# A decoder layer on one core: squares of x added by the matmul engine in the opening, other visit thresholds in the projections

## The chip, the core and the metric

The kernel runs on one core of a Trainium2 chip. In the profile PE is the matmul engine (PEld its weight loads), DVE the vector engine, ACT the scalar engine, POOL the general one, and SP the queue that issues nearly all DMAs. The metric is device time in microseconds (us) for one launch. Each engine works through its own list of instructions strictly in order, and waits where an operand or a buffer isn't ready; the lists are fixed when the program is built.

## The reference

One layer for 256 tokens of width 2048, all in float32:

```python
mod = jax.nn.silu(c) @ w_ada[l] + b_ada[l]
shift1, scale1, gate1, shift2, scale2, gate2 = jnp.split(mod, 6, axis=-1)
h = modulate(rms_norm(x, g_norm1[l]), shift1, scale1)   # h*(1+scale)+shift
p = h @ w_in[l]                                         # 2048 -> 12288
# retention on q,k,v,g and HGRN2 on q,f,i,g, both in chunks of 128 tokens,
# head norms, two output projections, gates, w_out
x = x + gate1[:, None, :] * (merged @ w_out[l])
h2 = modulate(rms_norm(x, g_norm2[l]), shift2, scale2)
u = causal_depthwise_conv(h2 @ w_up[l], conv_w[l], conv_b[l])
a, bgl = jnp.split(u, 2, axis=-1)
x = x + gate2[:, None, :] * ((jax.nn.silu(a) * bgl) @ w_down[l])
return rms_norm(x, g_final)
```

## The kernel before, in words

The width is cut into 16 pieces of 128, called k. A product with a float32 weight is made of three faster products: ACT copies a loaded weight tile `raw` into a rounded upper part `wh` (L176), DVE subtracts to get the rest `wl` (L181), and PE adds wh times the upper and the lower part of the activation and wl times the upper part. A tile pair wh, wl normally holds two k's by 512 columns. The pool `raw` has 11 buffers, and `wh` and `wl` have 4 each. All loads of weights stand in one queue, SP's, in the order of the program.

**The opening** (lines 305 to 430). The conditioning vector c is transposed on PE, put through Silu on ACT (L328, tile `col`), and spread over all partitions by 16 small matmuls in four groups of four (`spread`, L339, PSUM tiles `po`); ACT copies each group to the tile `sc` (L415, L427). Meanwhile x arrives transposed, in four tiles `xT`. Each is squared, folded and summed over the width by matmuls with a column of ones (`sums`, L375), which give the squared sum of each token in a `po` tile. `token_rstd` (L390, L391) takes the root on ACT and the reciprocal on DVE, and PE spreads the result (L395). For the root ACT needs another function table than for Silu; `sqrt_table` loads it (L402). Matmuls on ones (`idle`, L248) fill PE where it would stand. The tag `po` has four PSUM buffers: the fourth group of `spread` gets the buffer of the first, and waits until ACT has copied that one.

**Modulation.** The scale and the shift of one k are dot products of `sc` with rows of the conditioning weights: `ada_dot`, one `SCALAR_TENSOR_TENSOR` of 1024 elements a half on DVE (L507). For k=0 there are five of them (the last half is cut in two); the first two give the scale, the other three the shift. `times` multiplies x by the reciprocal (L497), `opening` makes z (L896), and `summed` makes h (L887). With h of k=0 PE begins the real products (`mm_plain`, L231). A second round of five dots leads to h of k=1 and to `mm_apart` (L242). All of this is pinned: it runs in the order in which it is written.

**The visits.** The projections to 14 column groups of 512 (`ATT`) begin before all k's are modulated. A planner (`visits`) goes round the groups; each visit takes the k's that a group has not yet had, and the number of k's that count as ready rises with the work done (a constant, one k for every 11 units). Groups 0 and 1 keep their PSUM banks to the end; every other visit ends with `take`: ACT copies the bank to SBUF the first time (L880), DVE adds it later (L882). The remaining dots, two scale and two shift dots for a k, run beside the visits. From here on nothing is pinned: a list scheduler decides the order on each engine, from its own estimate of when things are ready, when the program is built. After the visits come the heads, the output projections, the second norm, the convolution and the down projection; the change does not touch them.

Of the kernel before, what the change touches and what calls it, by code (L numbers as in the profile page):

```python
# [34 lines left out]
ADA_EVERY = 11  # L35
LAG = 2
NOSYNC = mybir.DependencyInfo(mybir.DependencyClass.NoSync, mybir.DependencyReason.DATA)
# [23 lines left out]
class Kernel:  # L61
# [106 lines left out]

    def upper(self, src, m, w, gain=None, shift=(0, 0)):

        raw = self.load(src, m, w)
        if gain is not None:
            self.pin(self.nc.vector.tensor_tensor(raw, raw, gain[:, None, :].to_broadcast([P, m, w]), ALU.mult))
        self.n += 1
        wh, wl = [self.part(n, m, w, at) for n, at in zip(("wh", "wl"), shift)]
        self.pin(self.nc.scalar.activation(wh, raw, AF.Copy))  # L176
        return raw, wh, wl
# [6 lines left out]

    def pieces(self, src, kts, gain=None, shift=(0, 0)):

        uppers = []
        for k in range(0, kts, 2):
            m = min(2, kts - k)

            while len(uppers) <= k // 2 + (gain is not None) and 2 * len(uppers) < kts:
                at = 2 * len(uppers)
                z = min(2, kts - at)
                uppers.append(self.upper(src[:, at : at + z, :], z, G, gain, shift))
# [48 lines left out]

    def idle(self, n):

        ps = self.pg()[0]
        for _ in range(n):
            self.pin(self.nc.tensor.matmul(ps[:, :P], lhsT=self.ones, rhs=self.ones, start=True, stop=True))  # L248

# [55 lines left out]
    def constants(self):  # L305
# [79 lines left out]
    def token_rstd(self, ps):  # L385
# [8 lines left out]
        for t in range(NT):  # L394
            self.pin(nc.tensor.matmul(ps[:, t * P : (t + 1) * P], lhsT=q[:, t : t + 1].to_broadcast([P, P]), rhs=self.ident, start=True, stop=True))  # L395
        self.idle(9)
        return ps
# [6 lines left out]
    def norm_x(self):  # L404

        nc = self.nc
        self.xT = self.load_x()
        ps = self.po()[:, :NT]
        for i, x in enumerate(self.xT):
            z = self.blk([P, 4, T], name="sq")  # L410
            if i == 0:
                self.pin(nc.vector.tensor_tensor(z, x, x, ALU.mult))
            elif i < 3:
                self.pin(nc.scalar.activation(z, x, AF.Square))
                self.pin(nc.scalar.activation(*self.silu.pop(0), AF.Copy))  # L415
            else:
                self.pin(nc.scalar.activation(z[:, :2, :], x[:, :2, :], AF.Square))
                self.pin(nc.vector.tensor_tensor(z[:, 2:, :], x[:, 2:, :], x[:, 2:, :], ALU.mult))
            if i < 3:
                self.pin(nc.vector.tensor_tensor(z[:, :2, :], z[:, :2, :], z[:, 2:, :], ALU.add))  # L420
                self.pin(nc.vector.tensor_tensor(z[:, 0, :], z[:, 0, :], z[:, 1, :], ALU.add))
            self.sums(ps, [z[:, j, :] for j in range(1 if i < 3 else 4)], i == 0, i == 3)
            if i == 0:
                for u in (2, 3):
                    self.spread(u)
        for part in self.silu:
            self.pin(nc.scalar.activation(*part, AF.Copy))  # L427
        return ps
# [417 lines left out]
    def run(self):  # L846
# [53 lines left out]
        gen = first(0)  # L900
        for _ in range(2):
            next(gen)
        rx = self.token_rstd(parts)
        rx_sb = c.tile([P, T], F32, name="rx_sb")
        next(gen)
        self.times(0, 1, rx)
        self.pin(nc.scalar.activation(rx_sb, rx, AF.Copy))
        z = opening(0)
        for _ in gen:
            pass  # L910
# [8 lines left out]
        for g in range(RESIDENT, FIRST):  # L919
            if g == RESIDENT:  # L920
                self.pin(nc.scalar.activation(hi, h, AF.Copy))
            uppers.append(self.upper(a["wa"][g][:, 0:1, :], 1, G))
        self.pin(nc.vector.tensor_tensor(lo, h, hi.bitcast(F32), ALU.subtract))
# [12 lines left out]
        for _ in gen:  # L936
            pass
        uppers = [self.upper(a["wa"][g][:, 1:2, :], 1, G) for g in range(RESIDENT)]
        hi, lo = act(1)[:, :T], act(1)[:, T:]
# [6 lines left out]
        for g in range(RESIDENT, FIRST):  # L946
            wh, wl = self.rest(self.upper(a["wa"][g][:, 1:2, :], 1, G))
            mms[g](ps[g], [(act(1), wh[:, 0, :], wl[:, 0, :])], False, True)
        begun = list(self.pieces(a["wa"][FIRST][:, 0:2, :], 2))
        for _ in range(2):  # L950
            next(ada[2])
# [446 lines left out]
```

## Time and profile before

| what | value |
|---|---|
| time, median of 3 runs | 1504.68 us (1504.5 to 1504.94) |
| time of the profiled execution | 1503.57 us |
| its span, first to last instruction | 1501.8 us |
| PE busy | 1485.5 us, 99% |
| DVE busy | 1210.5 us, 81% |
| ACT busy | 839.8 us, 56% |
| first real product (L231) starts at | 18.43 us |
| PE idle between 100 and 500 us | 2.34 us |

Times inside the profile count from the first instruction. A matmul of the opening in float32 shows as two passes, so eight matmuls of `sums` are 16 instructions there. A row of the timeline gives the start, the duration, the engine, the line, the tile written and the tiles read, and, in brackets, how long the engine stood before it and what ended that. Rows that follow each other with the same text are merged and counted.

### The profile page before, as it was taken

The numbers are of one execution on the slowest core, as the hardware profiler recorded it, in microseconds if no ns is written. First come the engines' busy times: TensorE is split into PE (matmuls) and PEld (weight loads), VectorE is DVE, ScalarE is ACT, GpSimd is POOL, SyncE is SP. The second block draws the span as 40 slices with busy tenths as digits, with TensorE's granted clock in tenths as the row PEclk, the third lists the DMA queues.
The fourth block names the chain that finished last, engine by engine and source line by source line (L and its number), as shares of the span: only waits on it lengthen the run. The fifth ranks groups of instructions, "written<-read, shape, count | busy, mean of one in ns | idle before, by whom it ended". The sixth has DMA issues, their size and how long they took to land.

```text
span 1501.8 us, 22826 instructions
## 1 busy us (share of the span) xinstructions
PE 1485.5 (99%) x8537; PEld 1274.6 (85%) x8537; DVE 1210.5 (81%) x1654; ACT 839.8 (56%) x1211; POOL 4.0 (0%) x8
## 2 busy tenths in 40 slices
PE   8999999999999999999999999999999999999997
PEld 7888889888888888888888888888888888888886
DVE  7899997999999877898978778778777769455694
ACT  5645546867775644445466555555555558344342
POOL 0000000000000000000000000000000000000000
PEclk9999999999999999999999999999999999999999
DMA  9999997688887889989847777777777666666551
GB/s 371 370 308 350 350 324 262 210 290 279 278 284 263 281 298 325 312 293 363 306 132 241 249 232 234 233 235 237 232 245 234 221 188 208 195 210 212 178 185 56
DMA packets 111455, 385.73 MB, mean 257 GB/s; under 512 B 12864, under 2 KB 13424, under 8 KB 111344
## 3 DMA queue, kind: packets, MB, share of 16 engines
q1 hardware_dynamic: 110448, 383.14, 76.3%
q8 instruction: 67, 1.10, 0.3%
q10 hardware_dynamic: 896, 1.13, 0.2%
q14 instruction: 44, 0.36, 0.1%
HBM read 382.11 MB, written 2.11 MB: 256 GB/s over the span
## 4 chain that ended last, share of the span: by engine, by line
PE 90%; DVE 5%; ACT 2%; DMA 1%; issue 1%; DVEq 0%; ACTq 0%; SPq 0%
PE pg L205 12%; PE pg L210 12%; PE pg L206 12%; PE po L1231 11%; PE pg L1231 11%; PE po L1233 5%; PE pg L1233 5%; PE pg L255 4%; PE po L206 3%; PE po L205 3%; PE po L210 3%; DVE wl L181 2%; PE pg L258 2%; DVE raw L507 1%; DVE p L882 1%
## 5 line engine op out<-in xcount | busy, mean ns | idle before, releaser
L181 DVE TENSOR_TENSOR wl<-raw,wh 128x1024 fp32r<-128x1024 f32 (+1 forms) x535 | 631.2, 1190 | 225.4 <-ACT wh L176 217.2
L176 ACT ACTIVATE wh<-raw 128x1024 fp32r<-128x1024 f32 (+1 forms) x535 | 545.8, 1032 | 468.1 <-PE pg L206 185.2
L507 DVE SCALAR_TENSOR_TENSOR raw<-raw,sc 128x1024 f32<-128x1024 f32 (+2 forms) x194 | 233.5, 1209 | 0.0
L205 PE MATMUL pg<-wh,hT 128*128 128x512 f32 x512 | 202.4, 396 | 3.7 <-ACT wh L176 2.6
L206 PE MATMUL pg<-wh,hT 128*128 128x512 f32 x512 | 199.8, 390 | 0.0
L1231 PE MATMUL po<-h2T,wh 128*128 128x512 f32 x704 | 175.8, 392 | 0.0
L1231 PE MATMUL pg<-h2T,wh 128*128 128x512 f32 x688 | 172.1, 392 | 0.0
L1231 PEld LDWEIGHTS po<-h2T,wh 128*128 128x128 f32 x704 | 125.7, 188 | 21.7
L1231 PEld LDWEIGHTS pg<-h2T,wh 128*128 128x128 f32 x688 | 122.8, 188 | 21.2
L210 PE MATMUL pg<-wl,hT 128*128 128x512 f32 x512 | 138.9, 390 | 0.3 <-DVE wl L181 0.3
L205 PEld LDWEIGHTS pg<-wh,hT 128*128 128x128 f32 x512 | 96.1, 188 | 25.3 <-ACT wh L176 4.9
L210 PEld LDWEIGHTS pg<-wl,hT 128*128 128x128 f32 x512 | 95.9, 188 | 21.0 <-DVE wl L181 0.9
L206 PEld LDWEIGHTS pg<-wh,hT 128*128 128x128 f32 x512 | 96.2, 188 | 19.4 <-DVE hT L436 0.3
L1233 PEld LDWEIGHTS po<-h2T,wl 128*128 128x128 f32 x704 | 93.4, 188 | 7.5
L1233 PEld LDWEIGHTS pg<-h2T,wl 128*128 128x128 f32 x688 | 91.3, 188 | 7.3
L1233 PE MATMUL po<-h2T,wl 128*128 128x256 f32 x704 | 94.5, 277 | 0.0
L1233 PE MATMUL pg<-h2T,wl 128*128 128x256 f32 x688 | 92.5, 277 | 0.0
L206 PE MATMUL pg<-wh,gs 128*128 128x512 f32 x176 | 68.6, 390 | 0.0
L205 PE MATMUL pg<-wh,gs 128*128 128x512 f32 x176 | 68.5, 389 | 0.0
L205 PE MATMUL po<-wh,gs 128*128 128x512 f32 x176 | 68.5, 389 | 0.0
L206 PE MATMUL po<-wh,gs 128*128 128x512 f32 x176 | 68.5, 389 | 0.0
L1244 ACT ACTIVATE u<-uy,convw 128x256 f32<-128x256 f32 x88 | 52.4, 595 | 28.7 <-DVE uy L1242 28.4
(273 smaller groups left out, 2033.9 us busy)
## 6 DMA issues: line engine op xcount, KB each, us to landing
raw<-in_wup SPq DMA_DIRECT2D x176, 512.0 KB, 4.5
raw<-in_wdown SPq DMA_DIRECT2D x88, 512.0 KB, 4.1
raw<-in_wa SPq DMA_DIRECT2D x79, 512.0 KB, 5.5
raw<-in_ada SPq DMA_DIRECT2D x64, 512.0 KB, 5.6
raw<-in_wab SPq DMA_DIRECT2D x64, 512.0 KB, 5.2
raw<-in_ada SPq DMA_DIRECT2D x62, 512.5 KB, 5.6
raw<-in_gate SPq DMA_DIRECT2D x32, 512.5 KB, 4.8
raw<-in_wk SPq DMA_DIRECT2D x32, 512.0 KB, 4.9
```

Of the source, the lines that this page charges most:

```text
L176: self.pin(self.nc.scalar.activation(wh, raw, AF.Copy))
L181: self.last = self.nc.vector.tensor_tensor(wl, raw, wh.bitcast(F32), ALU.subtract)
L205: nc.tensor.matmul(ps[t], lhsT=act[:, hi], rhs=wh, start=first and i == 0, stop=False)
L206: nc.tensor.matmul(ps[t], lhsT=act[:, lo], rhs=wh, start=False, stop=False)
L210: nc.tensor.matmul(ps[t], lhsT=act[:, hi], rhs=wl, start=False, stop=last and i == len(items) - 1)
L255: nc.tensor.matmul(ps[z], lhsT=wh[:, z * P : (z + 1) * P], rhs=act, start=first and i == 0, stop=False)
L258: nc.tensor.matmul(ps[z][:, :T], lhsT=wl[:, z * P : (z + 1) * P], rhs=act[:, :T], start=False, stop=last and i == len(items) - 1)
L507: dot = self.pin(nc.vector.scalar_tensor_tensor(raw[:, 0, :], raw[:, 0, :], 1.0, self.sc[:, at:to], ALU.mult, ALU.mult, accum_out=part[:, ...
L882: nc.vector.tensor_tensor(dst, dst, z, ALU.add)
L1231: self.pin(nc.tensor.matmul(ps[z], lhsT=wh[:, z * P : (z + 1) * P], rhs=act, start=kt == 0, stop=False, skip_group_check=bool(begun)))
L1233: nc.tensor.matmul(ps[z][:, :T], lhsT=wl[:, z * P : (z + 1) * P], rhs=act[:, :T], start=False, stop=kt == KT - 1, skip_group_check=bool(be ...
L1244: nc.scalar.activation(u, y, AF.Identity, bias=w[3], scale=w[2])
```

## The change

In the opening the order is written anew. The four squares are made as follows: tile 0 on DVE, folded twice; tile 1 on ACT, folded twice; tiles 2 and 3 half on ACT and half on DVE, tile 2 folded once and tile 3 not at all, so that PE sums two parts of tile 2 (four matmuls) and four of tile 3 (eight). The load of the root's table moves from behind Silu to behind the square of tile 1. `token_rstd` comes after one dot of k=0 where it came after two; the second dot follows the reciprocal, and the third follows the product with x. One filler matmul fewer stands after the spread of the reciprocal, and two new ones that read z stand before the first product. The first tiles of groups 2 and 3, and of 0 and 1 for k=1, get an offset of 8 bytes in their buffers (`COLS`), as later visits have. The weights of the second and third visit (`stock`) are loaded ahead of the dots of k=2. The thresholds of readiness are a table: 14, 24, 34, 45, ... units of work for k = 2, 3, 4, 5, ..., where the formula gave 13, 24, 35, 46, ... The plan has 46 visits where it had 47.

```diff
-LAG = 2
+READY = (14, 24, 34, *range(45, 156, 11))
...
-    def upper(self, src, m, w, gain=None, shift=(0, 0)):
+    def upper(self, src, m, w, gain=None, shift=(0, 0), raw=None):
-        raw = self.load(src, m, w)
+        raw = raw or self.load(src, m, w)
...
         self.pin(nc.scalar.activation(col, ps, AF.Silu))
-        self.sqrt_table()
...
-        self.idle(9)
+        self.idle(8)
         return ps
...
         ps = self.po()[:, :NT]
-        for i, x in enumerate(self.xT):
-            z = self.blk([P, 4, T], name="sq")
-            if i == 0:
-                self.pin(nc.vector.tensor_tensor(z, x, x, ALU.mult))
-            elif i < 3:
-                self.pin(nc.scalar.activation(z, x, AF.Square))
-                self.pin(nc.scalar.activation(*self.silu.pop(0), AF.Copy))
-            else:
-                self.pin(nc.scalar.activation(z[:, :2, :], x[:, :2, :], AF.Square))
-                self.pin(nc.vector.tensor_tensor(z[:, 2:, :], x[:, 2:, :], x[:, 2:, :], ALU.mult))
-            if i < 3:
-                self.pin(nc.vector.tensor_tensor(z[:, :2, :], z[:, :2, :], z[:, 2:, :], ALU.add))
-                self.pin(nc.vector.tensor_tensor(z[:, 0, :], z[:, 0, :], z[:, 1, :], ALU.add))
-            self.sums(ps, [z[:, j, :] for j in range(1 if i < 3 else 4)], i == 0, i == 3)
-            if i == 0:
-                for u in (2, 3):
-                    self.spread(u)
-        for part in self.silu:
-            self.pin(nc.scalar.activation(*part, AF.Copy))
+        zs = [self.blk([P, 4, T], name="sq") for _ in self.xT]
...
+        times(zs[0], self.xT[0])
+        fold(zs[0], 2)
+        fold(zs[0], 1)
+        self.pin(act(zs[1], self.xT[1], AF.Square))
+        self.sqrt_table()
+        fold(zs[1], 2)
+        fold(zs[1], 1)
+        self.sums(ps, [zs[0][:, 0, :]], True, False)
+        for u in (2, 3):
+            self.spread(u)
+        self.sums(ps, [zs[1][:, 0, :]], False, False)
+        for i in (2, 3):
+            self.pin(act(zs[i][:, low, :], self.xT[i][:, low, :], AF.Square))
+            times(zs[i][:, high, :], self.xT[i][:, high, :])
+            if i == 2:
+                fold(zs[i], 2)
+            spread_out()
+            self.sums(ps, [zs[i][:, j, :] for j in range(2 * i - 2)], False, i == 3)
+        while self.silu:
+            spread_out()
...
-        for _ in range(2):
-            next(gen)
+        next(gen)
         rx = self.token_rstd(parts)
         rx_sb = c.tile([P, T], F32, name="rx_sb")
         next(gen)
         self.times(0, 1, rx)
         self.pin(nc.scalar.activation(rx_sb, rx, AF.Copy))
+        next(gen)
         z = opening(0)
+        self.idle(2, z)
...
-            uppers.append(self.upper(a["wa"][g][:, 0:1, :], 1, G))
+            uppers.append(self.upper(a["wa"][g][:, 0:1, :], 1, G, shift=COLS))
...
         begun = list(self.pieces(a["wa"][FIRST][:, 0:2, :], 2))
+        stock = {g: self.load(a["wa"][g][:, 0:2, :], 2, G) for g in range(FIRST + 1, FIRST + 3)}
...
-                have = min(KT, 2 + int((work - LAG) / ADA_EVERY))
+                have = 2 + sum(work >= at for at in READY)
...
-            pieces = self.pieces(a["wa"][g][:, k : k + m, :], m, shift=visit(g))
+            pieces = self.pieces(a["wa"][g][:, k : k + m, :], m, shift=visit(g), raw=stock.pop(g, None))
```

How the lists of the engines move is shown at three places. A row is a line of the kernel, the operation, the tile written, the tiles read and the size.

The first place is the opening. On ACT, from Silu (`col`) to the copies of `sc`, before:

```order
L328 ACTIVATE col_99<-po_95 128x16
L402 ACT_TABLE_LOAD
L402 ACTIVATE warm_101<-eps_71 128x1
L414 ACTIVATE sq_138<-xT_114 128x1024
L415 ACTIVATE sc<-po_103 128x512
L414 ACTIVATE sq_145<-xT_115 128x1024
L415 ACTIVATE sc<-po_108 128x512
L417 ACTIVATE sq_152<-xT_116 128x512
```

And with the change:

```order
L328 ACTIVATE col_99<-po_95 128x16
L424 ACTIVATE sq_121<-xT_112 128x1024
L401 ACT_TABLE_LOAD
L401 ACTIVATE warm_128<-eps_71 128x1
L433 ACTIVATE sq_122<-xT_113 128x512
L419 ACTIVATE sc<-po_101 128x512
L433 ACTIVATE sq_123<-xT_114 128x512
L419 ACTIVATE sc<-po_106 128x512
```

Ahead of the first copy to `sc` there are now a square of 1024, the table, and a square of 512, where there were the table and a square of 1024. On DVE, from the last square to h of k=0, before:

```order
L418 TENSOR_TENSOR sq_152<-xT_116 128x512
L507 SCALAR_TENSOR_TENSOR raw_182,dot_32_181<-raw_182,sc 128x1024
L507 SCALAR_TENSOR_TENSOR raw_185,dot_32_181<-raw_185,sc 128x1025
L391 RECIPROCAL rq_191<-rq_191 128x2
L507 SCALAR_TENSOR_TENSOR raw_211,dot_39_210<-raw_211,sc 128x1024
L497 TENSOR_TENSOR xT_113<-xT_113,po_194 128x256
L507 SCALAR_TENSOR_TENSOR raw_218,dot_39_210<-raw_218,sc 128x512
L507 SCALAR_TENSOR_TENSOR raw_221,dot_39_210<-raw_221,sc 128x513
L887 TENSOR_SCALAR h_224<-z_216,dot_39_210 128x256
```

And with the change:

```order
L413 TENSOR_TENSOR sq_123<-xT_114 128x512
L520 SCALAR_TENSOR_TENSOR raw_184,dot_32_183<-raw_184,sc 128x1024
L390 RECIPROCAL rq_190<-rq_190 128x2
L520 SCALAR_TENSOR_TENSOR raw_206,dot_32_183<-raw_206,sc 128x1025
L510 TENSOR_TENSOR xT_111<-xT_111,po_193 128x256
L520 SCALAR_TENSOR_TENSOR raw_214,dot_39_213<-raw_214,sc 128x1024
L520 SCALAR_TENSOR_TENSOR raw_222,dot_39_213<-raw_222,sc 128x512
L520 SCALAR_TENSOR_TENSOR raw_225,dot_39_213<-raw_225,sc 128x513
L900 TENSOR_SCALAR h_228<-z_217,dot_39_213 128x256
```

The reciprocal stands one dot earlier, and so does the product with x: three dots instead of two stand between it and h.

The second place is ACT at the first visits, to groups 4, 5, 6 and 7, whose first upper parts are wh_383, wh_418, wh_441 and wh_461 before (wh_387, wh_424, wh_445 and wh_465 after) and whose copies to SBUF are p_173, p_174, p_175 before (p_175, p_176, p_177 after). Before:

```order
L176 ACTIVATE wh_383<-raw_381 128x1024
L880 ACTIVATE p_171<-pg_258 128x1024
L880 ACTIVATE p_172<-pg_278 128x1024
L518 ACTIVATE s_165<-dot_77_388 128x1
L519 ACTIVATE s_165<-gn_83,s_165 128x1
L880 ACTIVATE p_173<-pg_397 128x1024
L176 ACTIVATE wh_418<-raw_416 128x1024
L176 ACTIVATE wh_441<-raw_439 128x1024
L524 ACTIVATE t_166<-dot_81_412 128x1
L880 ACTIVATE p_174<-pg_423 128x1024
L176 ACTIVATE wh_461<-raw_459 128x1024
```

And with the change:

```order
L176 ACTIVATE wh_387<-raw_385 128x1024
L893 ACTIVATE p_173<-pg_262 128x1024
L176 ACTIVATE wh_424<-raw_391 128x1024
L893 ACTIVATE p_174<-pg_282 128x1024
L176 ACTIVATE wh_445<-raw_393 128x1024
L893 ACTIVATE p_175<-pg_405 128x1024
L893 ACTIVATE p_176<-pg_429 128x1024
L531 ACTIVATE s_167<-dot_80_396 128x1
L532 ACTIVATE s_167<-gn_83,s_167 128x1
L537 ACTIVATE t_168<-dot_84_420 128x1
L893 ACTIVATE p_177<-pg_450 128x1024
L176 ACTIVATE wh_465<-raw_463 128x1024
```

Before, the upper part for group 5 stood behind the copy of group 4; now that for group 7 stands behind the copy of group 6, and those for 5 and 6 stand ahead of the copies of 4 and 5.

The third place is DVE where `trig` (tiles `ang`, `n`) and `lower_bound` (`lbm`, `lbe`, `lb`) run beside the visits. Before:

```order
L181 TENSOR_TENSOR wl_1280<-raw_1277,wh_1279 128x1024
L584 TENSOR_TENSOR lbm_1734<-lbT 128x8
L181 TENSOR_TENSOR wl_1310<-raw_1307,wh_1309 128x1024
L586 TENSOR_TENSOR lbe_1735<-lbT,lbm_1734 128x8 x2
L507 SCALAR_TENSOR_TENSOR raw_1345,dot_217_1273<-raw_1345,sc 128x1025
L563 CAST ang_1352<-pos_1350 128x256
L588 TENSOR_TENSOR lbm_1734<-lbe_1735 128x8
L564 TENSOR_SCALAR ang_1352<-ang_1352,freq 128x256
L589 RECIPROCAL lbm_1734<-lbm_1734 128x8
L566 TENSOR_SCALAR n_1353<-ang_1352 128x256
L590 TENSOR_TENSOR lb<-lbe_1735,lbm_1734 128x8
L181 TENSOR_TENSOR wl_1361<-raw_1358,wh_1360 128x512
```

And with the change:

```order
L520 SCALAR_TENSOR_TENSOR raw_1280,dot_211_1210<-raw_1280,sc 128x1025
L576 CAST ang_1287<-pos_1285 128x256
L597 TENSOR_TENSOR lbm_1716<-lbT 128x8
L577 TENSOR_SCALAR ang_1287<-ang_1287,freq 128x256
L599 TENSOR_TENSOR lbe_1717<-lbT,lbm_1716 128x8 x2
L579 TENSOR_SCALAR n_1288<-ang_1287 128x256
L580 TENSOR_SCALAR n_1288<-n_1288 128x256
L583 SCALAR_TENSOR_TENSOR ang_1287<-n_1288,ang_1287 128x256 x3
L601 TENSOR_TENSOR lbm_1716<-lbe_1717 128x8
L584 TENSOR_SCALAR ang_1287<-ang_1287 128x256
L602 RECIPROCAL lbm_1716<-lbm_1716 128x8
L603 TENSOR_TENSOR lb<-lbe_1717,lbm_1716 128x8
```

Before, the later steps of `trig` (three products and the limit on `ang`) stand further on, one or two at a time between the visits' own rows; now both chains stand in one run, between a dot and the next `wl`.

More of the change, by code (lines that the diff above doesn't have):

```diff
@@ L183, in rest, with pieces @@
         return wh, wl
-    def pieces(self, src, kts, gain=None, shift=(0, 0)):
+    def pieces(self, src, kts, gain=None, shift=(0, 0), raw=None):
         uppers = []
@@ L193, in pieces @@
                 z = min(2, kts - at)
-                uppers.append(self.upper(src[:, at : at + z, :], z, G, gain, shift))
+                uppers.append(self.upper(src[:, at : at + z, :], z, G, gain, shift, raw if at == 0 else None))
             wh, wl = self.rest(uppers[k // 2])
@@ L242, in mm_apart, with idle @@
                     self.pin(nc.tensor.matmul(out, lhsT=w, rhs=act[:, cols], start=False, stop=False, skip_group_check=True))
-    def idle(self, n):
+    def idle(self, n, z=None):
         ps = self.pg()[0]
         for _ in range(n):
-            self.pin(self.nc.tensor.matmul(ps[:, :P], lhsT=self.ones, rhs=self.ones, start=True, stop=True))
+            self.pin(self.nc.tensor.matmul(ps[:, :P], lhsT=self.ones, rhs=self.ones if z is None else z[:, :P], start=True, stop=True))
     def mm_wide(self, ps, items, first, last, pair):
@@ L408, in norm_x, with times, fold, spread_out @@
         ps = self.po()[:, :NT]
-        for i, x in enumerate(self.xT):
-            z = self.blk([P, 4, T], name="sq")
-            if i == 0:
-                self.pin(nc.vector.tensor_tensor(z, x, x, ALU.mult))
-            elif i < 3:
-                self.pin(nc.scalar.activation(z, x, AF.Square))
-                self.pin(nc.scalar.activation(*self.silu.pop(0), AF.Copy))
-            else:
-                self.pin(nc.scalar.activation(z[:, :2, :], x[:, :2, :], AF.Square))
-                self.pin(nc.vector.tensor_tensor(z[:, 2:, :], x[:, 2:, :], x[:, 2:, :], ALU.mult))
-            if i < 3:
-                self.pin(nc.vector.tensor_tensor(z[:, :2, :], z[:, :2, :], z[:, 2:, :], ALU.add))
-                self.pin(nc.vector.tensor_tensor(z[:, 0, :], z[:, 0, :], z[:, 1, :], ALU.add))
-            self.sums(ps, [z[:, j, :] for j in range(1 if i < 3 else 4)], i == 0, i == 3)
-            if i == 0:
-                for u in (2, 3):
-                    self.spread(u)
-        for part in self.silu:
-            self.pin(nc.scalar.activation(*part, AF.Copy))
+        act, mul, add = nc.scalar.activation, ALU.mult, ALU.add
+        low, high = slice(0, 2), slice(2, 4)
+        zs = [self.blk([P, 4, T], name="sq") for _ in self.xT]
+        def times(z, x):
+            self.pin(nc.vector.tensor_tensor(z, x, x, mul))
+        def fold(z, n):
+            self.pin(nc.vector.tensor_tensor(z[:, :n, :], z[:, :n, :], z[:, n : 2 * n, :], add))
+        def spread_out():
+            self.pin(act(*self.silu.pop(0), AF.Copy))
+        times(zs[0], self.xT[0])
[18 more added lines that the diff above has]
+            spread_out()
         return ps
@@ L937, in run @@
             pass
-        uppers = [self.upper(a["wa"][g][:, 1:2, :], 1, G) for g in range(RESIDENT)]
+        uppers = [self.upper(a["wa"][g][:, 1:2, :], 1, G, shift=COLS) for g in range(RESIDENT)]
         hi, lo = act(1)[:, :T], act(1)[:, T:]
@@ L946, in run @@
         for g in range(RESIDENT, FIRST):
-            wh, wl = self.rest(self.upper(a["wa"][g][:, 1:2, :], 1, G))
+            wh, wl = self.rest(self.upper(a["wa"][g][:, 1:2, :], 1, G, shift=COLS))
             mms[g](ps[g], [(act(1), wh[:, 0, :], wl[:, 0, :])], False, True)
         begun = list(self.pieces(a["wa"][FIRST][:, 0:2, :], 2))
+        stock = {g: self.load(a["wa"][g][:, 0:2, :], 2, G) for g in range(FIRST + 1, FIRST + 3)}
         for _ in range(2):
```

## The prediction

> **What bounds the kernel now.** I read the page first: busy time and the chain of work that ended last.
>
> ```profile
> PE 1485.5 (99%) x8537; PEld 1274.6 (85%) x8537; DVE 1210.5 (81%) x1654; ACT 839.8 (56%) x1211; POOL 4.0 (0%) x8
> ...
> PE 90%; DVE 5%; ACT 2%; DMA 1%; issue 1%; DVEq 0%; ACTq 0%; SPq 0%
> ```
>
> PE is busy for 99% of the span and holds 90% of the chain. So a step elsewhere counts only where PE stands and waits for it. Second comes the list of PE's waits (what waits, for whom, total, times, longest).
>
> ```profile
> PE pg L205 <- ACT wh L176: 2.6, 2, 2.1
> PE pg L205 <- DVE p L882: 1.0, 2, 0.6
> PE po L242 <- ACT wh L176: 0.8, 1, 0.8
> ```
>
> Two places matter near the change: a wait of up to 2.1 for ACT's `wh` at one visit, and one of 0.8 ahead of the product with k=1. Third come the busy times by stretch.
>
> ```profile
> 34.40:36.50 2.10, 0.04 (x2) 0.02 (x1) 0.04 (x1) 2.04 (x3) 0.00 (x0) 1.00 1.03 412
> ...
> 100.00:500.00 400.00, 397.66 (x2868) 342.92 (x2867) 374.64 (x505) 255.39 (x372) 3.82 (x4) 1.00 0.85 290
> ```
>
> In 34.4 to 36.5 PE does nothing. Over the visits and what follows (100 to 500 us) it idles 400 - 397.66 = 2.34 us, and that is all that a better plan of visits could win there. Last I walked the timeline of the opening, up to 18.43 us, where the first real product starts.
>
> **The opening: when the reciprocal comes.** These rows carry the way from Silu to the sums.
>
> ```profile
> 6.12 1.28 ACT L402 ACT_TABLE_LOAD   x1
> 7.42 0.20 ACT L402 ACTIVATE warm<-eps 128x1 f32<-128x1 f32 x1
> 7.53 1.04 ACT L414 ACTIVATE sq<-xT 128x1024 f32<-128x1024 f32 x1
> 8.41 2.03 PE L339 MATMUL po<-ident,col 128*128 128x128 f32 x16
> 8.47 0.58 ACT L415 ACTIVATE sc<-po 128x512 f32<-128x512 f32 x1
> ...
> 10.28 0.51 PE L375 MATMUL po<-ones,sq 128*128 128x1 f32 x4
> 10.37 0.63 ACT L417 ACTIVATE sq<-xT 128x512 f32<-128x512 f32 x1
> 11.32 2.36 PE L375 MATMUL po<-ones,sq 128*128 128x1 f32 x20 [0.54 <-DVE sq L421]
> ```
>
> ACT loads the root's table at 6.12 (1.28), and its first copy to `sc` starts at 8.47. PE spreads c in two runs; the second, from 8.41, holds groups three and four, and the fourth must wait for that first copy. It never had to: the copy is done at 9.05, and half of 2.03 us after 8.41 is 9.4. The sums then start at 10.28 and end at 11.32 + 2.36 = 13.68.
>
> In the changed list the square of tile 1 goes first. It needs that tile:
>
> ```profile
> L361 SPq DMA_DIRECT2D xT<-in_xT x4: 391/422/432, 0.7 to 2.1; - x4
> DMA to landing us min/median/max: 3.8/5.6/6.8
> ```
>
> The four loads are issued 0.47 apart, and land 3.8 to 6.8 later, so I put the second at 1.2 + 5.2 = 6.4. Then ACT: 6.4 + 1.04 (square) + 1.28 (table) + 0.13 (warm, to the start of the next) + 0.53 (half a square, 0.63 less the overlap of 0.1 that 7.53 to 8.47 shows) = 9.4 for the start of the first copy, and 9.4 + 0.58 = 10.0 for its end. PE's fourth group waits from 9.4 to 10.0: the sums start at about 10.9, not 10.28.
>
> PE also adds more: 28 passes in place of 24 (tile 2 with four matmuls, two passes each). At 2.36 / 20 = 0.118 each they take 3.3 and end at 14.2. DVE doesn't hold them up: its folds and its half of tile 3 end at about 10.8. So the root and the reciprocal come **0.5 later**, not sooner: I take +0.5. Bounds: -0.1 if the fourth group doesn't wait (10.28 + 3.3 = 13.6), and +0.9 if tile 1 lands at the latest latency (1.2 + 5.6 to 6.8).
>
> By the Trainium skill ("ScalarE: Activation LUTs", "What ACT_TABLE_LOAD costs") a switch of tables costs the load of about 1283 ns and a drain of about 1380 ns, 2.66 us in all. The trace agrees with the load (1.28) but not with the drain: `warm` starts at 7.42, 0.02 after the load. By the page the first copy would end 1.4 later and the sum below would be 2.9 in place of 1.5.
>
> **The opening: from the reciprocal to h.**
>
> ```profile
> 13.72 0.26 ACT L390 ACTIVATE rq<-po,eps 128x2 f32<-128x2 f32 x1 [1.75 <-PE po L375]
> 14.02 0.17 DVE L391 RECIPROCAL rq<-rq 128x2 f32<-128x2 f32 x1
> 14.10 1.20 DVE L507 SCALAR_TENSOR_TENSOR raw<-raw,sc 128x1024 f32<-128x1024 f32 x1
> 14.33 1.20 PE L395 MATMUL po<-ident,rq 128*128 128x128 f32 x4
> 15.32 3.27 PE L248 MATMUL pg<-ones 128*128 128x128 f32 x18
> 15.56 0.42 DVE L497 TENSOR_TENSOR xT<-xT,po 128x256 f32<-128x256 f32 x1 [0.25 <-PE po L395]
> 15.90 0.69 DVE L507 SCALAR_TENSOR_TENSOR raw<-raw,sc 128x512 f32<-128x512 f32 x1
> 16.51 0.69 DVE L507 SCALAR_TENSOR_TENSOR raw<-raw,sc 128x513 f32<-128x513 f32 x1
> 17.32 0.41 DVE L887 TENSOR_SCALAR h<-z,dot 128x256 f32<-128x256 f32 x1
> 18.43 3.62 PE L231 MATMUL po<-h,raw 128*128 128x256 f32 x16
> ```
>
> Before: root 13.72, reciprocal 14.02, spread 14.33, product with x 15.56, dots four and five 15.90 and 16.51, h 17.32. The third dot (14.10, 1.20) filled the 1.2 us in which DVE waited for the spread. In the changed list the second dot stands in that hole, and the third comes behind the product with x. The first dot alone is ahead of the reciprocal, and DVE then waits for the root with nothing to do, from about 12.2 to 14.5. So one dot of 1.20 moves from a free place onto the path: **+1.2** (it is 1024 elements; 1.1 to 1.3 with what overlaps). h is 0.5 + 1.2 = 1.7 later, at 19.0.
>
> PE's start moves less. The fillers ended at 18.43, 0.7 after h, so h may be 0.6 late for nothing: 19.0 + 0.41 + 0.05 gives 19.5 for L231, about +1.0. The eight fillers and the two that read z (each two passes, 3.27 / 18 = 0.18 a pass, 20 x 0.18 = 3.6) run from about 15.8 and end at 19.4, beside DVE's dots: I cost them at nothing. If h came sooner they would show, with 0.2 to 0.4.
>
> But PE's start isn't what counts. The next place where PE stands is L242:
>
> ```profile
> 20.28 1.22 DVE L507 SCALAR_TENSOR_TENSOR raw<-raw,sc 128x1024 f32<-128x1024 f32 x1
> 25.14 0.41 DVE L887 TENSOR_SCALAR hT<-z,dot 128x256 fp32r<-128x256 f32 x1
> 25.69 2.14 PE L242 MATMUL po<-hT,wh 128*128 128x256 f32 x16 [0.78 <-ACT wh L176]
> ```
>
> Between h of k=0 (17.32) and h of k=1 (25.14) DVE runs its list with no hole but 0.6 us for ACT's `hT` and `wh`, which wait for h themselves; five dots of the second round stand in it. It moves as a whole, so L242 moves from 25.69 to 27.4. PE's own work up to there moves by 1.0, and its wait of 0.8 grows to 1.5. Term: **+1.7**, from 1.0 (-0.1 + 1.1) to 2.2 (0.9 + 1.3).
>
> **The offset of 8 bytes.** The first matmuls on tiles without it, and later ones on tiles with it:
>
> ```profile
> L222 PE MATMUL pg<-hT,wh 128*128 128x256 f32 x16 | 4.0, 283 | 0.0
> ...
> L222 PE MATMUL pg<-hT,wh 128*128 128x256 f32 x16 | 3.8, 278 | 0.0
> ```
>
> 283 against 278 ns. The 48 matmuls from L242 on gain 5 ns each: **-0.2**, at most -0.4 with the 24 ahead of it, at least 0.
>
> **The stall at the first visits.**
>
> ```profile
> 33.35 1.07 PE L210 MATMUL pg<-wl,hT 128*128 128x512 f32 x4
> 36.48 0.50 PE L205 MATMUL pg<-wh,hT 128*128 128x512 f32 x1 [2.06 <-ACT wh L176]
> ...
> 34.46 1.02 ACT L880 ACTIVATE p<-pg 128x1024 f32<-128x1024 f32 x1 [0.80 <-PE pg L210]
> 35.38 2.00 ACT L176 ACTIVATE wh<-raw 128x1024 fp32r<-128x1024 f32 x2
> 38.86 0.30 ACT L524 ACTIVATE t<-dot 128x1 f32<-128x1 f32 x1 [1.49 <-DVE raw L507]
> ```
>
> PE ends group 4 at 34.42. ACT must first copy the bank out (34.46), then make `wh` for group 5 (35.38), and PE goes on at 36.48. With the change these two rows are in the good order for groups 5 and 6, whose weights come two loads earlier. But for group 7 the list has them the other way: the copy of group 6 stands ahead of wh_465, and ACT takes its list in order. So PE ends group 6, waits for a copy and an upper part, and loses the same 2.06. **The stall moves two visits on: 0.** The delay of 1.7 isn't swallowed either, since this wait starts from PE's own end. Bounds: -0.5 to 0. The two loads go past four dots' loads of k=2 in SP's queue; at 412 GB/s each is 1.3 us, so those land up to 2.6 later. Their last dot was done at 38.86, and group 7 needs k=2 only after 41.9 + 2.7: hidden, and if the cover were gone, under 1 us.
>
> **The plan of visits.** One visit fewer saves a DVE addition (about 1.2 us), off PE's path. Thresholds a unit earlier or later move which k a visit takes, not how many products PE does. What it can win is the 2.34 of idle time; what it can lose is priced with the first rival, 2.7. The wins and losses are near each other, so I take **0**.
>
> **Sum.** 1.7 - 0.2 + 0 + 0 = +1.5 us. The profiled execution took 1503.57 (span 1501.8 and 1.8 around it), so it would be 1505.1; the median of the runs lies 1.1 higher, at 1504.68, and the forecast for that is **1506.2**. Ends: 1.0 - 0.4 - 0.5 - 2.3 = -2.2 gives 1502.5; 2.2 + 2.7 = +4.9 gives 1509.6.
>
> **Rivals.**
>
> *Slower: the run of trig and lower bound on DVE.* One dot and all small steps now stand in one run between two `wl` of the visits.
>
> ```profile
> 120.00:150.00 30.00, 2.49 (x7) 0.84 (x2) 1.00 0.95 341
> ...
> 91.21 1.83 DVE L181 TENSOR_TENSOR wl<-raw,wh 128x512 fp32r<-128x512 f32 x2
> ...
> 94.45 0.84 PE L210 MATMUL pg<-wl,hT 128*128 128x512 f32 x3
> ```
>
> The steps of `ang` alone are 2.49 us on DVE, spread over 24 us before; with those of the lower bound and less overlap, I put the run at 3.0. With a dot (1.2) and a `wl` (1.2) DVE needs 5.4 for a piece that PE eats in 24 matmuls, 2.7 us. The piece two before it is as heavy, and the one between gives 1.5 back: DVE loses about 4.1 of its lead. Its lead there decides: before, a `wl` done at 93.0 was used at 94.45, 1.4 ahead. From a lead of 4.1 on it costs nothing; at 1.4 it costs 4.1 - 1.4 = 2.7. For it: DVE is the second busiest engine here. Against it: there is less DVE work ahead of the run than before, so the lead should be larger, and the data come early. Time: 1506.2 + 2.7 = 1508.9. Chance 0.19.
>
> *It does what it says.* The fourth group doesn't wait, so the reciprocal is 0.1 earlier, and the visits lose 1.4 less. For it: the waits of 100 to 500 us are made by DVE and ACT, which the plan relieves. Against it: the copy to `sc` stands behind the table. The third dot still costs 1.2: 1504.68 - 0.1 + 1.2 - 0.2 - 1.4 = 1504.2. Chance 0.16.
>
> *The stall is gone.* ACT finds wh_465 in time after all, and the plan wins its 2.34: 1.0 - 0.2 - 2.1 - 2.3 = -3.6, so 1501.1. Against it: a list isn't reordered. Chance 0.10.
>
> *The drain.* The page's rule would make the opening 1.4 later: 1507.6. Against it: the row at 7.42. Chance 0.04.
>
> **How the numbers follow.** The forecast has 0.51. About 0.2% (3.0 us) is what a measurement of this kernel can tell from no change. Past it lie only the run on DVE (slower, 0.19) and the stall gone (faster, 0.10); the forecast, the second and the last rival stay within (0.71). The range 1503.0 to 1508.9 leaves out the stall gone and the worse half of the first rival. The forecast's own range is 1505.0 to 1507.5.
>
> **What would show it.** The root on ACT at 14.2, the third dot behind the product with x, h at 19.0, L242 at 27.4 (each +0.3 or less). PE idle for 2.1 between the visits to groups 6 and 7, and none between 4 and 5. The forecast is wrong in the opening if the root comes before 13.7 or h before 18.0; wrong at the visits if there is no such gap, or if PE's idle time from 100 to 500 us leaves 1.0 to 3.5.

## The result, and the profile after

The changed kernel takes 1512.89 us (median of 4 runs, 1512.01 to 1516.16), the kernel before 1504.63. The ratio is 1.0059, with an interval of 1.0041 to 1.0076: it is 8.3 us slower. The forecast was 1506.2, with a range up to 1508.9; the result lies outside it. The profiled execution took 1516.16 (span 1514.4), the longest of the four, and is 12.6 longer in span than the one of before. The profiled execution of before lies 1.1 under its median and this one 3.3 over its own, so about 4.3 of the 12.6 is a difference between executions and 8.3 is the change.

First the page and PE's waits after the change (what waits, for whom, total, times, longest), then a stretch of the span (its length, the busy time of PE, its weight loads, DVE, ACT and POOL, then the granted clock, the DMA share and GB/s).

```profile
PE 1492.6 (99%) x8543; PEld 1282.0 (85%) x8543; DVE 1209.3 (80%) x1651; ACT 836.6 (55%) x1207; POOL 4.0 (0%) x8
...
PE 93%; DVE 3%; ACT 1%; DMA 1%; issue 1%; DVEq 0%; ACTq 0%
```

```profile
PE pg L255 <- DVE p L277: 4.7, 1, 4.7
PE pg L205 <- ACT wh L176: 3.0, 2, 2.1
PE po L221 <- ACT wh L176: 1.1, 1, 1.1
```

```profile
100.00:500.00 400.00, 391.87 (x2823) 338.50 (x2821) 364.98 (x491) 245.22 (x359) 3.81 (x4) 0.99 0.84 287
```

PE still holds the chain, now 93% of it. The longest wait is one that was 0.3 before: 4.7 us at L255, for DVE's addition L277. The wait for `wh` at the first visits is there as before, 2.1. The idle time from 100 to 500 us, on which the prediction put 1.0 to 3.5, is 8.1 us (400 - 391.87), where it was 2.34.

L255 and L258 are the products of the wide groups behind the visits. A group fills two PSUM tiles `pg` in turn, four pieces each (a piece is a row of 8 matmuls at L255 and one of 8 at L258). ACT (L276) and DVE (L277) must copy them out before the next group can begin; the text below calls that place the change of tiles (the expectations say change of banks). Beside them run the heads: the products L776 and L778 (L763 and L765 before), then ACT's squared sums (L782, L769), a root with a table load (L352, L353), and the next gate. Here is that place in the trace, after:

```profile
368.06 0.29 ACT L544 ACTIVATE gate<-dot 128x1 f32<-128x1 f32 x1 [1.11 <-DVE raw L520]
...
368.23 1.10 PE L258 MATMUL pg<-hT,wl 128*128 128x256 f32 x8
...
370.73 0.39 PE L778 MATMUL po<-p,a 128*128 128x128 f32 x2
...
371.18 1.28 ACT L352 ACT_TABLE_LOAD   x1
...
374.15 0.59 ACT L276 ACTIVATE p<-pg 128x512 f32<-128x512 f32 x1
...
375.06 0.66 DVE L277 TENSOR_TENSOR p<-p,pg 128x512 f32<-128x512 f32 x1
...
375.86 3.75 PE L255 MATMUL pg<-hT,wh 128*128 128x512 f32 x8 [4.75 <-DVE p L277]
...
379.41 1.91 PE L258 MATMUL pg<-hT,wl 128*128 128x256 f32 x8
...
381.12 2.41 PE L255 MATMUL pg<-hT,wh 128*128 128x512 f32 x8
```

```profile
375.16:381.99 6.83, 6.13 (x19) 5.19 (x20) 2.88 (x7) 5.83 (x8) 0.95 (x1) 0.50 0.43 175
```

And before:

```profile
358.61 1.28 ACT L353 ACT_TABLE_LOAD   x1
...
359.41 0.39 PE L765 MATMUL po<-p,a 128*128 128x128 f32 x2
...
359.56 2.09 PE L255 MATMUL pg<-hT,wh 128*128 128x512 f32 x8
...
364.30 0.58 ACT L276 ACTIVATE p<-pg 128x512 f32<-128x512 f32 x1
...
364.92 0.69 DVE L277 TENSOR_TENSOR p<-p,pg 128x512 f32<-128x512 f32 x1 [0.26 <-ACT p L276]
...
365.66 2.12 PE L255 MATMUL pg<-hT,wh 128*128 128x512 f32 x8 [0.32 <-DVE p L277]
```

Before, two pieces of the same group lie between the last product of the heads and the change of PSUM tiles. They take until 365.3 (365.66 less the wait of 0.32), and ACT has time for squares, root and both tables ahead of L276. After, the last L258 of the group is done ahead of the heads' last products, and the next matmul needs the tiles at once. But ACT starts its copy only at 374.15. It has worked without a hole since 368.06, where a gate had waited 1.11 for a dot of DVE, and from 371.18 on a table load (1.28), the root, four squared sums and another gate stand ahead of the copy in its list. PE stands for 4.75, until 375.86, and runs at half clock behind that (the granted clock is 0.50 from 375.16 to 381.99, second fence: 3.75, 1.91 and 2.41 for rows that take 2.12, 1.09 and 1.99 otherwise).

PE's busy time in two stretches after, and in the second of them before (in the first it was busy throughout):

```profile
60.00:100.00 40.00, 39.61 (x234) 35.03 (x233) 36.98 (x48) 22.76 (x35) 0.00 (x0) 1.00 0.96 327
100.00:200.00 100.00, 97.71 (x574) 86.02 (x573) 97.94 (x134) 52.66 (x78) 0.95 (x1) 1.00 0.94 333
```

```profile
100.00:200.00 100.00, 99.13 (x605) 87.60 (x603) 97.88 (x135) 53.00 (x79) 1.91 (x2) 1.00 0.97 344
```

Where the 12.6 of the two spans went, from these rows and the granted clock:

| place | us |
|---|---|
| up to L242 (25.69 to 28.08) | +2.4 |
| wait at the first visits: 2.06, moved from group 5 to group 7 | 0 |
| half clock in the 3.4 us behind that wait (matmuls start 0.43 apart in place of 0.23) | +1.5 |
| PE idle 60 to 200 us (0.87 before, 2.68 after) | +1.8 |
| wait at the heads (0.32 before, 4.75 after) | +4.4 |
| half clock in the 6.8 us behind it (3.75 + 1.91 + 2.41 where 2.12 + 1.09 + 1.99 would stand) | +2.9 |
| rest, not traced (the other waits from 200 to 500 us make -0.1 of it) | -0.4 |

### The profile page after: what moved, and what is told of

It reads as the page before. It is cut to its first block, busy times and chain, and to the rows that moved or that the text cites. A ratio compares the mean times of both kernels' runs of the same rounds, so it can differ in the third digit from the quotient of the medians.

```text
span 1514.4 us, 22812 instructions
## 1 busy us (share of the span) xinstructions
PE 1492.6 (99%) x8543; PEld 1282.0 (85%) x8543; DVE 1209.3 (80%) x1651; ACT 836.6 (55%) x1207; POOL 4.0 (0%) x8
## 4 chain that ended last, share of the span: by engine, by line
PE 93%; DVE 3%; ACT 1%; DMA 1%; issue 1%; DVEq 0%; ACTq 0%
PE pg L205 13%; PE pg L206 13%; PE pg L210 13%; PE po L1246 11%; PE pg L1246 10%; PE po L1248 5%; PE pg L1248 5%; PE pg L255 4%; PE po L210 3%; PE po L206 3%; PE po L205 3%; PE pg L258 2%; DVE raw L520 1%; DVE wl L181 1%; PE pg L222 1%
## 5 line engine op out<-in xcount | busy, mean ns | idle before, releaser
L210 PEld LDWEIGHTS pg<-wl,hT 128*128 128x128 f32 x512 | 96.2, 188 | 20.3
L255 PE MATMUL pg<-hT,wh 128*128 128x512 f32 x256 | 66.9, 405 | 4.7 <-DVE p L277 4.7
```

The source lines that it names most:

```text
L210: nc.tensor.matmul(ps[t], lhsT=act[:, hi], rhs=wl, start=False, stop=last and i == len(items) - 1)
L255: nc.tensor.matmul(ps[z], lhsT=wh[:, z * P : (z + 1) * P], rhs=act, start=first and i == 0, stop=False)
```

## The experiments

Two theories stood at first. **A**: the loss is the wait at the heads, and the table of thresholds makes it. **B**: it is the opening, and the later waits follow from its delay.

**Opening alone, thresholds alone, and the change without either.** The first kernel is the one before with the new `norm_x`, the place of the table, the order of the dots and the fillers, as in the change:

```diff
+        times(zs[0], self.xT[0])
+        fold(zs[0], 2)
+        fold(zs[0], 1)
+        self.pin(act(zs[1], self.xT[1], AF.Square))
+        self.sqrt_table()
...
-        for _ in range(2):
-            next(gen)
+        next(gen)
         rx = self.token_rstd(parts)
```

The second has only this:

```diff
-LAG = 2
+READY = (14, 24, 34, *range(45, 156, 11))
...
-                have = min(KT, 2 + int((work - LAG) / ADA_EVERY))
+                have = 2 + sum(work >= at for at in READY)
```

The third is the change with these lines undone; the fourth is the change with the opening of before.

> Only the opening of the change (squares, table, order of the dots, fillers); thresholds, offset and early loads as before. Theory A (the loss sits mainly at the heads, where the new thresholds put the change of the two PSUM banks right behind the second products of the heads): no wait above 1 us there, L242 at 28 instead of 25.7, so +2.4, about 1507.0. Theory B (the loss sits in the opening, and the later waits and half clocks follow from it): most of the +8 is here, 1510 or more. The prediction's own term for the opening gives +1.7, 1506.3.

> Only the table of thresholds in place of the formula; opening, offset and loads as before. Theory A: the heads end right at the change of banks, PE stands there for 4 to 5 us (0.5 before), and a window of half clock may follow (1.7 us for each 3.4): +4.4 to +7, so 1509 to 1511.6. Theory B: no loss, 1504 to 1505, and the wait at the heads, if there, is made good later. The prediction's term for the plan gives 0, 1504.6.

> The change without its table of thresholds (formula as before). Theory A: the heads lie two pieces ahead of the change of banks again, no long wait there; what is left is the opening, 1507.0, up to 1508.6 where the wait at the visit to group 7 costs a window of half clock. Theory B: 1510 or more, as with the whole change.

> The change without its opening (squares, table, dots and fillers as before); thresholds, offset and early loads stay. Theory A: the wait at the heads is there, +4.4 to +7, so 1509 to 1511.6. Theory B: 1504 to 1506.

| kernel | median | before | ratio (interval) | longest wait at L255 |
|---|---|---|---|---|
| opening alone | 1506.15 | 1504.34 | 1.0012 (1.0002 to 1.0021) | 0.3 |
| thresholds alone | 1513.36 | 1504.34 | 1.0059 (1.0043 to 1.0076) | 4.8 |
| no thresholds | 1506.38 | 1504.34 | 1.0012 (1.0003 to 1.0022) | 0.3 |
| old opening | 1512.31 | 1504.34 | 1.0054 (1.0039 to 1.0069) | 4.8 |

The last column stands in the list of PE's waits, here of the thresholds alone and then of the opening alone:

```profile
PE pg L255 <- DVE p L277: 4.8, 1, 4.8
```

```profile
PE pg L255 <- DVE p L277: 0.3, 1, 0.3
```

B falls. The two kernels with the table have the wait and 8 to 9 us; the two without have neither. The opening costs 1.8 (0.3 to 3.2), though L242 was not at 28 there but at 26.7 (below). Theory A's +4.4 to +7 for the thresholds was low beside the median, +9.0 (interval 6.5 to 11.4): it left out the new waits at the visits (PE idles 2.29 from 100 to 200 us there, 0.87 before). The early loads and the offset make no difference that can be seen (1506.38 against 1506.15). The parts don't add up to the whole by their medians: 1.8 and 9.0 are 10.8, and the change measured 8.3. Its interval, 6.2 to 11.4, allows both, and no run here settles it.

**The heads moved, both ways.** Does the wait come from where the heads stand, or do the thresholds cost their 8 us by the order of the visits in any case (theory C)? The background work has a rate; I moved the heads by it alone. The whole change, with the heads a little slower:

```diff
-                    self.pace(0, 14.0, 24)
+                    self.pace(0, 14.5, 24)
```

and the kernel before, with 13.0 in that place. In the first, PE's list has two pieces of the group behind the heads' last product again; in the second, none.

> The whole change, with one number more: the background work of the first heads is given 14.5 us for 24 steps where it had 14, so that their last products come two pieces ahead of the change of banks again. Theory A (the heads at the change of banks): the wait of 4.9 there falls to under 1 us and the half clock behind it goes; what is left is the opening (+1.8) and about 1 us at the visits, so 1507 to 1508, 5 or more under the whole change. Theory C (the thresholds cost their 8 to 9 us by the order of the visits, and the wait at the heads only collects it): 1511 to 1513, the lost time shows elsewhere.

> The kernel before, with 13 us for 24 steps in place of 14, nothing else: the heads' last products now stand right ahead of the change of banks, as in the change, with the old thresholds. Theory A: PE stands 3.5 to 5 us there, and one or two windows of half clock follow (1.7 each): +4 to +8, 1508 to 1512. Theory C: 1504 to 1505.

The change with the heads moved takes 1507.72 beside 1505.01 before: ratio 1.0018 (1.0009 to 1.0027), 2.7 us in place of 8.3. The kernel before with its heads at the change of tiles takes 1506.49: ratio 1.0015 (1.0005 to 1.0024), +1.5. PE's waits of the first and of the second:

```profile
PE pg L255 <- DVE p L277: 0.3, 1, 0.3
```

```profile
PE pg L255 <- DVE p L277: 2.9, 1, 2.9
```

The wait goes and comes with the place of the heads, whatever the thresholds. C falls; A holds, with two misses in the second kernel. Its wait is 2.9, not 3.5 to 5: only one squared sum and an upper part stand between the root and the copy there (four squared sums and the gate in the change). And it wins at another place: PE's idle time from 200 to 300 us is 1.05 before and 0.00 here, since the same rate moves other work too. 2.9 - 0.3 - 1.05 leaves 1.5 of waits. That this equals the +1.5 of the medians (0.8 to 3.6) is in part luck, for the profiled execution has half clock behind the wait as well, where the row took 2.12 before:

```profile
368.28 3.37 PE L255 MATMUL pg<-hT,wh 128*128 128x512 f32 x8 [2.88 <-DVE p L277]
```

**The opening taken apart.** The new squares alone (with the dots in the old order), and the new order of the dots alone:

```diff
-        for _ in range(2):
-            next(gen)
+        next(gen)
         rx = self.token_rstd(parts)
...
+        next(gen)
         z = opening(0)
+        self.idle(2, z)
```

> The kernel before with the new squares, sums and place of the table alone; the dots stay in the old order (two ahead of the reciprocal, the third behind it). With full clock from about 5 us on: reciprocal at 14.2, h 3.3 behind it as before (the third dot lies beside PE's spread), so 17.5, L242 at 25.9. If instead the squares carry the whole delay, h is at 18.3 and L242 at 26.7, as with the full opening.

> The kernel before with the new order of the dots and fillers alone (one dot ahead of the reciprocal, the third behind the product with x); squares, sums and table as before. If the third dot on the path carries the opening's whole delay (theory A): reciprocal at 14.0 as before, h 4.1 behind it in place of 3.0 to 3.3, so 18.1 to 18.2, L242 at 26.5 to 26.7. If the reciprocal really comes sooner for want of the second dot: below 13.8, and L242 at 25.9.

One execution each, read for its timeline: 1503.58 and 1505.68. The rows of the new squares alone:

```profile
6.40 2.05 PE L338 MATMUL po<-ident,col 128*128 128x128 f32 x16
...
14.41 0.17 DVE L390 RECIPROCAL rq<-rq 128x2 f32<-128x2 f32 x1 [1.14 <-ACT rq L389]
...
17.37 0.41 DVE L900 TENSOR_SCALAR h<-z,dot 128x256 f32<-128x256 f32 x1
```

Of the dots alone:

```profile
5.80 2.05 PE L339 MATMUL po<-ident,col 128*128 128x128 f32 x16
...
13.66 0.17 DVE L391 RECIPROCAL rq<-rq 128x2 f32<-128x2 f32 x1 [1.10 <-ACT rq L390]
...
17.77 0.41 DVE L887 TENSOR_SCALAR h<-z,dot 128x256 f32<-128x256 f32 x1
```

And of both, the opening alone of the first experiment:

```profile
5.88 2.05 PE L338 MATMUL po<-ident,col 128*128 128x128 f32 x16
...
9.71 1.16 PE L338 MATMUL po<-ident,col 128*128 128x128 f32 x8 [0.45 <-ACT sc L419]
...
13.93 0.26 ACT L389 ACTIVATE rq<-po,eps 128x2 f32<-128x2 f32 x1 [2.29 <-PE po L374]
14.22 0.17 DVE L390 RECIPROCAL rq<-rq 128x2 f32<-128x2 f32 x1 [2.29 <-ACT rq L389]
...
18.34 0.41 DVE L900 TENSOR_SCALAR h<-z,dot 128x256 f32<-128x256 f32 x1
...
26.71 2.15 PE L242 MATMUL po<-hT,wh 128*128 128x256 f32 x16 [1.32 <-DVE hT L900]
```

The way from the reciprocal to h is 2.96 with the old order (14.41 to 17.37) and 4.11 with the new one (13.66 to 17.77; 14.22 to 18.34): the third dot costs 1.15. The new squares cost 0.15 and 0.48 in the two executions shown: from PE's first spread of c to the reciprocal it is 8.34 in the last fence, where it was 7.86 before (6.16 to 14.02), and 8.01 in the first one (6.40 to 14.41). (In two more executions with early full clock it is 8.26, without thresholds, and 8.77, with the heads moved, where PE's fourth group waits 0.86 for ACT's copy: so 0.15 to 0.9 in all.) With the dots alone the reciprocal is at 13.66, under the 13.8 that the expectation set for a gain. It isn't one: c landed sooner in that execution, PE's spread began at 5.80, and 13.66 - 5.80 is 7.86, as before. The way to h is 4.1, as the third dot makes it, and L242 is at 26.15 (26.5 to 26.7 less the 0.36 of c).

**The wait at the first visits.** Before, the upper part for group 5 stands behind the copy of group 4 in ACT's list; two early loads shift that to group 7. With three, and the offset, in the kernel before:

```diff
+        stock = {g: self.load(a["wa"][g][:, 0:2, :], 2, G) for g in range(FIRST + 1, FIRST + 4)}
...
-            pieces = self.pieces(a["wa"][g][:, k : k + m, :], m, shift=visit(g))
+            pieces = self.pieces(a["wa"][g][:, k : k + m, :], m, shift=visit(g), raw=stock.pop(g, None))
```

> The kernel before with the offset of 8 bytes and with three weights loaded early (groups 5, 6 and 7, where the change loads two); opening and thresholds as before. The upper part of every group up to 8 then stands ahead of the copy of the group before it in ACT's list. If the wait of 2.1 at the first visits comes from that order alone, it is gone: PE idle under 0.8 between 30 and 60 us, 1502.0 (-2.3). If the weights themselves come too late (the DMA engines are full up to 60 us), PE waits there for DMA in place of ACT, and the time stays at 1504.

1503.17 (11 runs), ratio 0.9990 (0.9981 to 0.9999): 1.8 us faster than before by the medians, and the only kernel here whose interval lies under 1, if barely. PE idles 0.60 from 30 to 60 us, where it was 2.06:

```profile
30.00:60.00 30.00, 29.40 (x134) 24.17 (x134) 24.04 (x34) 23.35 (x32) 0.00 (x0) 1.00 1.03 408
100.00:200.00 100.00, 98.22 (x600) 86.80 (x599) 97.74 (x134) 52.97 (x79) 1.91 (x2) 1.00 0.98 344
```

PE's waits there are for ACT, not for DMA, though the DMA engines are as full as before (1.03): the order of the list was the cause, not the weights. Not all is kept. From 100 to 200 us PE idles 1.78 where it was 0.87 (at 102 us an upper part stands behind a step `t` of ACT that waits for a dot, 1.3). So the waits alone come to 0.6 less. The half clock that follows the wait of 2.06 in some executions (last section) is not in this one; whether that is the rest of the 1.8 was not measured.

**Two tries to go further.** One gives the heads 13 us as above and shifts them off the change of tiles by a second rate; the other adds a faster rate for the dots of the visits:

```diff
-                    self.pace(0, 14.0, 24)
+                    self.pace(0, 13.0, 24)
...
-        self.pace(0, 143.0, 88)
+        self.pace(0, 155.0, 88)
...
-        self.pace(1, 4, ADA_EVERY / 2)
+        self.pace(1, 4.6, ADA_EVERY / 2)
```

(the last pair in the second kernel alone).

> The kernel of the three early loads, with two rates of background work altered: 13 us for 24 steps in place of 14 (this took the waits at 280 and 288 us away where it was tried alone), and 155 us for 88 steps in place of 143, which brings the last products of the heads two pieces ahead of the change of banks again. Theory A: no wait over 1 us at the heads, none at 280 and 288 us: 1.2 under the kernel of the three early loads, 1502.0 where that has 1503.2. Rival: the heads' other work meets another change of banks or visit, 1503 to 1505.

> The kernel of the run beside it, and the dots of the visits are given 4.6 us for 5.5 steps in place of 4, so that each comes a little sooner in DVE's list. If the waits of 1.4 at 102 us and 0.65 at 147 us come from upper parts that stand behind a step of ACT that waits for such a dot, they shrink by 1 to 1.5 together: 1500.5 to 1501. If the sooner dots push the lower parts of the weights back on DVE, PE waits for those in their place: 1502 or more.

1503.34, ratio 0.9992 (0.9983 to 1.0001), and 1504.78, ratio 1.0003 (0.9994 to 1.0012). Neither gains on the three early loads. In the first the waits at 280 and 288 us are gone (idle 0.00 from 200 to 300 us) and a new one of 0.6 for a lower part stands at 354 us. In the second the waits at 102 and 147 us are gone, and three for lower parts have come:

```profile
PE pg L210 <- DVE wl L181: 1.1, 3, 0.6
```

That is the rival written down for it: sooner dots push the lower parts back on DVE. But it is not all. From 100 to 500 us PE idles 2.08 in the second kernel and 2.81 in the first, so the sooner dots won there on balance. They lost at 44 us, where PE waits 1.50 in place of 0.58:

```profile
44.82 0.50 PE L205 MATMUL pg<-wh,hT 128*128 128x512 f32 x1 [1.50 <-ACT wh L176]
```

In the first kernel ACT copies a group out at 40.11 and then makes the step `t`, which needs a dot; in the second `t` stands ahead of that copy, waits 1.57 for the dot, and the copy (43.25) and the upper part behind it (44.16, 42.70 in the first) come late. It is the order of the list again. How the 1.4 between the two medians divides among these places was not measured.

## Why the prediction was wrong

**The step that failed** is the plan of visits: "Thresholds a unit earlier or later move which k a visit takes, not how many products PE does ... so I take 0". It counted what PE does and what idles from 100 to 500 us, and took it that the work behind the visits keeps its place. Without the new opening this term, put at 0, measured +8 to +9 (1512.31 with the offset and the early loads, 1513.36 alone, beside 1504.34). The change leaves the code of the heads as it is, but not their place: they are background work that begins when the groups of a head are complete. By the plan of before 36 k's of other groups are then still to come for the first head and 33 for the second; by the new table 39 and 37. The heads' last products moved by two pieces, onto the change of tiles, and cost 4.4 and a half clock behind it. This could be seen in PE's list before any run, by reading which L255 follows the last L778 and which tile it writes. (How 3 or 4 k's of the plan become these two pieces was not traced; that the heads' place decides was shown by moving them.) The bounds of that term couldn't hold it: -2.34 is the idle time that was there already, and +2.7 is the price of a wait within the visits. Half clock behind a wait had no term at all; it cost about 2.9 at the heads.

**The opening** came about by the mechanism that was forecast. Forecast: reciprocal +0.5, third dot +1.2, L242 +1.7. Measured at a like start: reciprocal +0.15 to +0.9, third dot +1.15; in time +1.8 (0.3 to 3.2). The interval is wide, so that 1.8 agrees with 1.7 shows little by itself. Step by step the numbers are shifted. With full clock from 5 us on (the opening alone) PE's fourth group waits for ACT's copy, as said (0.45, until 9.71; forecast 0.6, until 10.0), and the root comes at 13.93, forecast 14.2; h at 18.34, forecast 19.0; L242 at 26.71, +1.0. That is less than +1.7 because before, half clock stretched PE's spread of the reciprocal: the way to h was 3.30 in that execution, and 2.96 where the spread ran at full clock (the new squares, the thresholds alone). In the profiled execution of the change full clock came only at 9.93, and the rows read

```profile
6.36 3.62 PE L338 MATMUL po<-ident,col 128*128 128x128 f32 x16
...
15.30 0.26 ACT L389 ACTIVATE rq<-po,eps 128x2 f32<-128x2 f32 x1 [2.43 <-PE po L374]
...
19.70 0.41 DVE L900 TENSOR_SCALAR h<-z,dot 128x256 f32<-128x256 f32 x1
...
28.08 2.10 PE L242 MATMUL po<-hT,wh 128*128 128x256 f32 x16 [1.41 <-DVE hT L900]
```

3.62 for 16 passes, where it was 2.05: root at 15.30, h at 19.70, L242 at 28.08. The forecast of 27.4 lay between the two executions. Over all profiled executions L242 starts at 27.35 in the mean with the whole new opening (four, 26.71 to 28.08) and at 25.94 with the old one (seven, 25.23 to 26.83): +1.4. Counted from PE's first spread of c, in those with full clock before 7 us, it is 20.8 to 21.5 with the new opening (three) and 19.2 to 20.3 with the old (five), +1.5 in the mean. The prediction did not see that the moment at which full clock comes goes with 1.1 of L242 between executions with the same opening (last section), not much less than the term.

**The offset and the early loads** were costed at -0.2 and 0; together they show no difference (1506.38 with them, 1506.15 without).

**The stall** moved from group 5 to group 7 with the same 2.06, as forecast. The half clock behind it, which is in this execution and not in that of before, was not in the forecast:

```profile
42.08 1.02 ACT L893 ACTIVATE p<-pg 128x1024 f32<-128x1024 f32 x1 [0.28 <-PE pg L210]
43.00 1.05 ACT L176 ACTIVATE wh<-raw 128x1024 fp32r<-128x1024 f32 x1
...
44.10 0.80 PE L205 MATMUL pg<-wh,hT 128*128 128x512 f32 x1 [2.06 <-ACT wh L176]
```

**The rival on DVE** (the run of trig and lower bound, 0.19) had the place right and the engine wrong. The run stands from 126.9 to 130.4, and PE does wait there, 1.1 us, but for ACT: the table of the lower bound stands ahead of an upper part. (ACT had stood 3.37 for a dot of DVE just before, until 126.97; what each of the two costs was not separated.)

```profile
127.70 1.28 ACT L600 ACT_TABLE_LOAD   x1
...
129.12 1.04 ACT L176 ACTIVATE wh<-raw 128x1024 fp32r<-128x1024 f32 x1
...
130.22 0.39 PE L221 MATMUL po<-hT,wh 128*128 128x256 f32 x1 [1.10 <-ACT wh L176]
```

No lower part is late: PE's waits after the change have no row for DVE's `wl`. That wait is in all four kernels with the table (the change, thresholds alone, old opening, heads moved), and in none without; it is the larger part of the +1.8 at the visits.

"It does what it says", "the stall is gone" and "the drain" did not come: the reciprocal isn't sooner, the wait is there, and `warm` starts at 8.51, right behind the table's end at 8.50.

## What to carry to other kernels

A change of a planner's numbers moves everything that is timed by the plan, behind it too: after each such change, look at where background work meets the places at which a buffer must be free, and read which instruction follows it in the list of the bound engine. Where a copy that frees a PSUM tile stands behind a table load, a root and sums of other work in its engine's list, two pieces of cover decided over 4.4 us here. And before a long dot is moved behind a wait, see whether it filled that wait: a dot of 1.2 in a hole of 1.2 is free, behind it it costs 1.15.

## What the runs showed of the hardware

PE's clock is granted in steps of 3.41 us, and the steps lie differently against the program in each execution. Whether a wait cost half clock afterwards went with how much of it fell into one step. The wait of 2.06 at the first visits is in ten of the thirteen profiled executions. In six, 1.9 to 2.06 of it fell into one step, PE was busy for 0.40 to 0.45 of that step, and the next one ran at half clock; in four, 1.5 to 1.8 of it fell into one step, PE was busy for 0.47 to 0.55, and the clock stayed. Here are a step with its next, of the change and then of before:

```profile
40.65:44.06 3.41, 1.39 (x7) 0.81 (x5) 0.82 (x2) 2.61 (x5) 0.00 (x0) 1.00 1.04 413
44.07:47.48 3.41, 3.38 (x8) 2.71 (x9) 3.40 (x6) 2.42 (x4) 0.00 (x0) 0.50 1.03 406
```

```profile
34.68:38.09 3.41, 1.61 (x7) 1.35 (x8) 1.63 (x2) 2.69 (x3) 0.00 (x0) 1.00 1.03 413
38.10:41.50 3.40, 3.40 (x17) 2.82 (x16) 1.87 (x3) 2.26 (x4) 0.00 (x0) 1.00 1.05 409
```

1.39 of 3.41 is 0.41, and the clock of the next step is 0.50; 1.61 is 0.47, and it is 1.00. So the same wait costs 2.1, or 3.6 with the 1.5 of half clock behind it. And full clock came at 4.0 to 6.9 us in ten executions, at 9.9 to 10.6 in three: with the old opening L242 is at 25.69 before, where it came at 3.97, and at 26.83 in the thresholds alone, where it came at 10.61. By the Trainium skill ("TensorE: Matmul & The Clock Gate", "What's actually happening") the window is 3413 ns and runs free of the program; the trace agrees (3.413, and another phase in each execution). By its rule in "HAM oscillation — how this bites in real kernels" only gaps over about 3.4 us are to be avoided. The measurement differs and decides: here 2.06 is enough, where nearly all of it falls within one window.
